# A spare weight load moved ahead of a lot's last loads, its split placed behind later products, and no spare pairs in the second layer

## The chip, the cores and the metric

The kernel runs on one core of a Trainium2 chip. A time is the device time of one execution of the whole program in microseconds (us). Times of a kernel are the median of several executions; one more execution was profiled.

## The reference

The reference is an encoder trunk of two layers on 512 tokens of width 1024, all in fp32:

```
for i in range(DEPTH):                       # DEPTH = 2
    h = rms_norm(x, g_mix_pre[i])
    proj = h @ w_in[i]                       # queries, keys, values, memory queries
    ...                                      # layer 0: banded attention, layer 1: full attention
    o = jnp.concatenate([tok, mo], axis=-1) @ w_o[i]
    x = x + rms_norm(o, g_mix_post[i])
    h = rms_norm(x, g_ffn_pre[i])
    gu = h @ w_gate_up[i]                    # 1024 x 5632
    f = (jax.nn.silu(gu[..., :D_FF]) * gu[..., D_FF:]) @ w_down[i]     # D_FF = 2816
    x = x + rms_norm(f, g_ffn_post[i])
```

## The kernel before

**Products.** TensorE (PE) has to reach fp32 accuracy from fp32r operands, so every operand is split into a high part (ScalarE, ACT, line 318, here called `whi` for weights) and a low part (VectorE, DVE, line 322, `wlo`), and each product is three matmuls: high by high, low by high, high by low. A weight of 512 KB is loaded by the queue of SyncE (SP) into a tile of 128x1024, named `raw`, `ru` or `rb` by its pool, and split from there; `rs` is a half of that size.

**The feed-forward part** (`ffn`, line 984) runs over 22 blocks of 128 hidden columns in four lots, `LOTS` = 0-2, 2-8, 8-14, 14-22. The two lots of six blocks (`SEVEN`; here the first and the second lot of a layer) save multiplications by the scheme that makes a 2x2 block product from seven products. For each hidden block, `body` (line 1151) makes gate and up (PE lines 1131 to 1133); its end is `s` (DVE line 1185), which `keep_hidden` splits into the pair `f` (ACT line 1007, DVE line 1008), the stationary operand of the down product.

**The down product of such a lot** (`down`, line 1310; matmuls on lines 1257 to 1259) needs seven combinations of the four blocks b11, b12, b21, b22 of the down weight. `down_load` (line 1269) loads them in four steps, each as a main tile and an `rs`; sums are made by accumulating DMAs on GpSimd's (POOL's) queue: t1 = b11+b12, t2 = b22+t1, t3 = b12+b22, t4 = b21+t2. Step 0 and step 1 are issued during the lot's last two blocks, step 2 (t3) with the first product A11, step 3 (t4 and b22) after A12. In `down` follow six products of 18 matmuls each: A12 (with b21), S2 (t2), S1 (t1), S3 (t3), S4 (b22), A22 (t4). Each has six steps of three matmuls; the last hidden block enters A12 in its fifth step. Before each, `pairs` splits the main tile and the `rs`.

**Spare work.** Some weights of layer 1 are used once as they are, so layer 0 splits four of them ahead and stores the parts to DRAM, where the mixer of layer 1 reads them back (`unit` looks them up in `self.pairs`). The list is `self.todo`, set at line 1554: four query weights and then four output weights. Twice in each `down`, `spare` either takes the next weight, loads it and splits it in two halves into tiles `c` (high) and `s` (low), or stores the parts that the call before made. `ahead` (line 231), called four times in `ffn_out`, does the same with whole tiles. In layer 0, four calls of each kind make the pairs of the four query weights. The list isn't emptied, so in layer 1 the same calls load, split and store the four output weights, which nothing reads afterwards.

**Who sets the order.** PE's order is that of the code. The orders of ACT, DVE, POOL and SP are set by the tile framework's planner when the kernel is built, from the data's dependences and its own estimate of when they are ready; each of these engines then runs its list strictly in that order. `queue` ties the DMAs that it issues to each other, so that they keep the code's order on their queue. `raw` tiles have three buffers.

Of the kernel before, what the change touches and what calls it, by code (L numbers as in the profile page):

```python
# [203 lines left out]
class Trunk:  # L204
# [290 lines left out]
    def rope(self, l, x, t, n, z):  # L495
        return self.rope_b(x, t, n, z) if l else self.rope_a(x, t, n)
# [487 lines left out]
    def ffn(self, l, pools, forms, late, done):  # L984
# [3 lines left out]
        nc = self.nc  # L988
        f32r = lambda pool, shape, tag, n=1: pool.tile(shape, F32R, tag=tag, name=tag, bufs=n)
        F, o, gu, tmp = {}, [], pools["gu"], None  # L990
        w, raw, st, turn, kept, forms_due, ends = {}, {}, {}, {}, {}, [], {}

        def units(f):
            w[f] = [self.unit(self.a["wgu"][l, f, b]) for b in range(2)]
# [82 lines left out]
        def queue(eng, *args, **kw):  # L1077
            with self.tc.issue_after(ends[eng]) if eng in ends else nullcontext():
                ends[eng] = eng.dma_start(*args, **kw).ins
# [140 lines left out]
        for k in range(2):  # L1220
            c = slice(512 * k, 512 * k + 512)
# [30 lines left out]
        def times(ps, h, name, pr, steps, fresh):  # L1252
            mm = nc.tensor.matmul
            for i, t in steps:
                lh, ll = block(h["lot"], name, 0, i, t), block(h["lot"], name, 1, i, t)
                rh, rl = [pr[i // 2][z][:, i % 2 * 512:i % 2 * 512 + 512] for z in range(2)]
                mm(ps[t], lh, rh, start=fresh and i == 0, stop=False, skip_group_check=True)  # L1257
                mm(ps[t], lh, rl, start=False, stop=False, skip_group_check=True)  # L1258
                mm(ps[t], ll, rh, start=False, stop=i == HALF - 1, skip_group_check=True)  # L1259
# [27 lines left out]
            down_load(h, 2)  # L1287
            times(h["x"], h, "A11", h["w"], BY_UNIT[:4], True)

        def spare():  # L1290
            if l == 0 and "rope" not in turn:
                turn["rope"] = 1
                self.axial(tmp.tile([P, 10 * HD], F32, tag="rope", name="rope", bufs=1), queue, ends)
            if self.stores:
                for dst, src in self.stores:
                    queue(nc.sync, dst, src)
                self.stores = []
            elif self.todo:
                name, *at = self.todo.pop(0)
                x = self.wraw.tile([P, 1024], F32, tag="raw", name="raw", bufs=3)  # L1300
                queue(nc.sync, x, self.a[name][tuple(at)])
                self.pairs[(name, *at)] = y = [self.dram.tile([P, 1024], F32, name="pair", tag="_".join(map(str, (name, z, *at))))
                                               for z in range(2)]
                for z in range(2):
                    c = slice(512 * z, 512 * z + 512)
                    hi, lo = temp("c"), temp("s")
                    self.split(hi.bitcast(F32R), lo.bitcast(F32R), x[:, c])
                    self.stores += [(y[0][:, c], hi), (y[1][:, c], lo)]

        def down(h):  # L1310

            x = h["x"]
            due()
            out_of(x, 0, 0)
            w = pairs(h["b21"])
            z = [self.tagged("s"), self.tagged("s")]
            times(z, h, "A12", w, BY_UNIT, True)
            down_load(h, 3)
            spare()
            out_of(z, 0, 0)  # L1320
            w = pairs(h["t2"])
            times(x, h, "S2", w, BY_UNIT, False)
            out_of(x, 0, 1, True)
            w = pairs(h["t1"])
            y = [self.tagged("pv"), self.tagged("t")]
            times(y, h, "S1", w, BY_ROW, True)
            spare()
            out_of(y, 1, 1)
            w = pairs(h["t3"])
            times(x, h, "S3", w, BY_ROW, False)  # L1330
            out_of(x, 1, 1, True)
            w = pairs(h["b22"])
            times(y, h, "S4", w, BY_ROW, False)
            out_of(y, 0, 1)
            w = pairs(h["t4"])
            times(x, h, "A22", w, BY_ROW, False)
            out_of(x, 1, 0)

        for c, (f0, f1) in list(enumerate(LOTS))[1:]:
# [40 lines left out]
            if c in SEVEN:  # L1380
                down(head)
# [114 lines left out]
    def run(self):  # L1496
        tc, nc, a = self.tc, self.nc, self.a
        with ExitStack() as top:
            top.enter_context(tc.manual_schedule(engines={mybir.EngineType.PE}))
            glob = self.glob = self.pool(top, "glob")  # L1500
            self.small = self.pool(top, "small")
            self.wraw = self.pool(top, "wraw")
            self.whl = self.pool(top, "whl")
            self.ps, self.nbank, self.turns = self.psum(top, "ps"), 0, ["s0", "s1", "s2"]
            dram = self.dram = top.enter_context(tc.tile_pool(name="dram", bufs=1, space=bass.MemoryType.DRAM))
            xs = [[dram.tile([P, D], F32, name=f"x{i}{t}", tag=f"x{i}{t}") for t in range(NT)] for i in range(3)]
            self.spill = dram.tile([P, 2, KD, NMEM], F32, name="smem", tag="smem")
            x0 = [a["x"][0, t * P:(t + 1) * P] for t in range(NT)]
            out = [a["out"][0, t * P:(t + 1) * P] for t in range(NT)]

            cst = self.cst = glob.tile([P, 2 * P], F32, name="cst")
            self.ident = cst[:, :P]
            self.ropet = cst[:, P:2 * P].rearrange("p (a t d) -> p a t d", a=2, d=16)
            self.gcol = glob.tile([P, 2, KD], F32, name="gcol")
            self.sink, self.nsink = [glob.tile([P, NH], F32, name=z) for z in ("sink", "nsink")]
            self.gt = glob.tile([P, 2, 2, NT, HD], F32, name="gt")
            self.identr = glob.tile([P, P], F32R, name="identr")
            self.mhalf = glob.tile([P, 4], F32, name="mhalf")
            nc.gpsimd.memset(self.mhalf, -0.5)

            hs = [ExitStack() for _ in range(DEPTH + 1)]
            self.slab(hs[0], 0)
            hb, norm = ExitStack(), ExitStack()
            self.hbuf = self.pool(hb, "h0", side="right")
            self.norm_pool(norm)
            late = {}
            for l in range(DEPTH):
                last = l == DEPTH - 1
                mix = ExitStack()
                tokp = self.pool(mix, f"tok{l}")  # L1530
                core = ExitStack()
                mkp = self.pool(core, f"mk{l}")
                self.mT = tokp.tile([P, 2, KD, NMEM], F32R, tag="tok", name="mT", bufs=1)
                if l == 0:
                    late = self.start(mkp)
                norm.close()
                self.core = self.pool(core, f"core{l}")
                self.more = self.core if l else None
                self.mixer(l, mkp, late, tokp)
                self.more = None  # L1540
                core.close()
                hb.close()

                keep, fts, norm = ExitStack(), ExitStack(), ExitStack()
                if l == 0:
                    self.gap(keep, "gap0", 56)
                forms = Forms(self, self.pool(keep, f"keep{l}", side="right"),
                              self.pool(fts, f"forms{l}", side="right"))
                self.norm_pool(norm)
                self.hT = None  # L1550
                late = self.mix_out(l, forms, x0 if l == 0 else xs[1], xs[2 * l])
                mix.close()
                if not last:
                    self.todo = [("wq", 1, c, z) for c in (2, 3) for z in range(2)] + [("wo", 1, 0, u) for u in range(4)]
                ff = ExitStack()
                pools = dict(ff=ff, gu=self.pool(ff, f"gu{l}"), norm=norm, forms=fts)
                get, fs, o, head = self.ffn(l, pools, forms, late, keep.close)
                norm = ExitStack()
                if not last:
                    self.gap(hs[l + 1], "gap1", 8)  # L1560
                    self.slab(hs[l + 1], 1, side="right")
                    hb = ExitStack()
                    self.hbuf = self.pool(hb, f"h{l + 1}", side="right")
                self.norm_pool(norm)
                late = self.ffn_out(get, a["wd"][l], fs, o, head, a["g_ffn_post"][l], a["g_mix_pre"][1], xs[2 * l], out if last else xs[1], None if last else self.new_rs())
                ff.close()
                if l == 0:
                    hs[0].close()
            norm.close()
            for z in hs[:0:-1]:  # L1570
                z.close()
# [30 lines left out]
```

## Time and profile before

| | us |
|---|---|
| median of 3 executions | 1102.06 (1100.99 to 1105.8) |
| profiled execution, device time | 1100.04 |
| profiled execution, span from its first to its last instruction | 1098.3 |
| PE busy | 1065.9 (97%) |
| DVE busy | 899.5 (82%) |
| ACT busy | 697.7 (64%) |
| POOL busy | 251.8 (23%) |
| HBM read and written | 149.04 MB and 18.87 MB |
| mean granted clock of PE | 0.993 |

In the rows that follow, `A:B` is a stretch in us from the start of the span. In a row of such stretches stand its length, PE's busy time in it (with the number of matmuls that touch it), the granted clock (1.00 is full speed), the share of time in which the DMA engines were busy, and GB/s. A row of the timeline has an instruction's start, its duration, engine, source line, operation, what it writes and reads, and in square brackets the idle time of its engine before it with what ended it. `SPq` and `POOLq` rows are the issues of DMAs; q0 is the queue of POOL's DMAs and q1 that of SP's. A matmul starts 0.23 us after the one before it when nothing holds it; its row is longer since matmuls overlap.

### The profile page before, as it was taken

What the parts mean: (1) busy time and instruction counts of PE and PEld (TensorE: products, weight loads), DVE (VectorE), ACT (ScalarE), POOL (GpSimd) and SP (SyncE); (2) the same over time, 40 slices, a digit from 0 to 9 for tenths busy, and PEclk for the clock granted to TensorE, in tenths of its full rate; (3) what the DMA queues carried; (4) which work ended last, traced back from release to release, by engine and by line L of the source; (5) the groups of instructions that cost most, each with busy time, mean ns of one, the idle gap of its engine ahead of it and who ended that gap; (6) DMA issues with size and microseconds to landing.
All of it is one profiled execution on the core that took longest, in us unless ns stands there. A gap on an engine that the chain in (4) does not pass through costs nothing.

```text
span 1098.3 us, 20016 instructions
## 1 busy us (share of the span) xinstructions
PE 1065.9 (97%) x7364; PEld 973.1 (89%) x7364; DVE 899.5 (82%) x1567; ACT 697.7 (64%) x1435; POOL 251.8 (23%) x405
## 2 busy tenths in 40 slices
PE   9999999999989989999999999999999999999997
PEld 7899878999969979998898888778999799799986
DVE  7889876978978979985888998767979888899955
ACT  7679975766636645664557888756766456556641
POOL 5673331111221100001443543312011011100001
PEclk9999999999989999999999999999999999999999
DMA  8721008357967983328743200145469968943283
GB/s 327 261 75 41 22 20 288 116 135 209 221 226 188 231 254 105 116 91 317 240 159 116 77 17 24 39 165 194 94 172 230 267 160 238 223 164 104 72 281 115
DMA packets 57555, 175.51 MB, mean 160 GB/s; under 512 B 6641, under 2 KB 7025, under 8 KB 57329
## 3 DMA queue, kind: packets, MB, share of 16 engines
q1 hardware_dynamic: 47952, 152.86, 40.9%
q0 software_dynamic: 9216, 20.98, 11.3%
q8 instruction: 58, 0.95, 0.3%
q10 hardware_dynamic: 288, 0.40, 0.1%
q14 instruction: 41, 0.33, 0.1%
HBM read 149.04 MB, written 18.87 MB: 153 GB/s over the span
## 4 chain that ended last, share of the span: by engine, by line
PE 75%; DVE 9%; DMA 6%; ACT 4%; issue 2%; POOL 2%; SPq 0%; DVEq 0%; POOLq 0%; ACTq 0%
PE ps L1131 11%; PE ps L1132 11%; PE ps L1133 11%; PE ps L309 8%; PE ps L308 8%; PE ps L310 8%; PE tp L673 3%; PE ps L1258 2%; PE ps L1259 2%; PE ps L1257 2%; DVE wlo L322 2%; PE o L687 2%; DMA rs<-rs 2%; PE o L688 2%; PE s L612 1%
## 5 line engine op out<-in xcount | busy, mean ns | idle before, releaser
L318 ACT ACTIVATE whi<-raw 128x512 fp32r<-128x512 f32 (+3 forms) x186 | 145.8, 803 | 99.6 <-issue 24.7
L322 DVE TENSOR_TENSOR wlo<-raw,whi 128x512 fp32r<-128x512 f32 (+3 forms) x182 | 162.7, 910 | 37.1 <-ACT whi L318 36.5
L1132 PE MATMUL ps<-hrows,wlo 128*128 128x256 f32 x640 | 176.2, 275 | 0.0
L1131 PE MATMUL ps<-hrows,whi 128*128 128x256 f32 x640 | 176.2, 275 | 0.0
L1133 PE MATMUL ps<-hrows,whi 128*128 128x256 f32 x640 | 176.1, 275 | 0.0
L308 PE MATMUL ps<-whi,hrows 128*128 128x256 f32 (+2 forms) x432 | 143.8, 333 | 0.0
L309 PE MATMUL ps<-wlo,hrows 128*128 128x256 f32 (+2 forms) x432 | 137.8, 319 | 1.6 <-DVE wlo L322 1.5
L310 PE MATMUL ps<-whi,hrows 128*128 128x256 f32 (+2 forms) x432 | 137.8, 319 | 0.0
L1132 PE MATMUL ps<-a,wlo 128*128 128x256 f32 x480 | 132.1, 275 | 0.0
L1131 PE MATMUL ps<-a,whi 128*128 128x256 f32 x480 | 132.1, 275 | 0.0
L1133 PE MATMUL ps<-a,whi 128*128 128x256 f32 x480 | 132.1, 275 | 0.0
L1131 PEld LDWEIGHTS ps<-hrows,whi 128*128 128x128 f32 x640 | 120.2, 188 | 0.5
L1132 PEld LDWEIGHTS ps<-hrows,wlo 128*128 128x128 f32 x640 | 120.1, 188 | 0.5
L1133 PEld LDWEIGHTS ps<-hrows,whi 128*128 128x128 f32 x640 | 120.2, 188 | 0.0
L663 POOL TENSOR_SCALAR p<-p,rd 128x256 f32<-128x256 f32 (+2 forms) x128 | 77.4, 626 | 102.1 <-DVE rd L660 58.3
L1132 PEld LDWEIGHTS ps<-a,wlo 128*128 128x128 f32 x480 | 90.1, 188 | 0.2
L1131 PEld LDWEIGHTS ps<-a,whi 128*128 128x128 f32 x480 | 90.1, 188 | 0.2
L1133 PEld LDWEIGHTS ps<-a,whi 128*128 128x128 f32 x480 | 90.1, 188 | 0.0
L309 PEld LDWEIGHTS ps<-wlo,hrows 128*128 128x128 f32 x432 | 81.4, 188 | 7.3 <-DVE wlo L322 2.4
L310 PEld LDWEIGHTS ps<-whi,hrows 128*128 128x128 f32 x432 | 81.1, 188 | 5.5 <-DVE hrows L336 0.3
L308 PEld LDWEIGHTS ps<-whi,hrows 128*128 128x128 f32 x432 | 81.3, 188 | 5.1
L318 ACT ACTIVATE whi<-rb 128x1024 fp32r<-128x1024 f32 x56 | 59.5, 1063 | 27.0 <-PE ps L1259 18.5
(231 smaller groups left out, 2854.1 us busy)
## 6 DMA issues: line engine op xcount, KB each, us to landing
raw<-in_wgu_dram SPq DMA_DIRECT2D x48, 512.0 KB, 4.7
rb<-in_wgu_dram SPq DMA_DIRECT2D x40, 512.0 KB, 4.4
raw<-in_wo_dram SPq DMA_DIRECT2D x20, 512.0 KB, 3.6
raw<-in_wd_dram SPq DMA_DIRECT2D x18, 512.0 KB, 4.6
raw<-in_wq_dram SPq DMA_DIRECT2D x16, 512.0 KB, 4.9
rb<-in_ws_dram SPq DMA_DIRECT2D x16, 512.0 KB, 6.6
rs<-in_ws_dram SPq DMA_DIRECT2D x28, 256.0 KB, 5.4
xt<-x SPq DMA_DIRECT2D x12, 512.0 KB, 4.4
```

The source lines that it names most:

```text
L308: mm(out, lh, rh, start=first, stop=False)
L309: mm(out, lh, rl, start=False, stop=False)
L310: mm(out, ll, rh, start=False, stop=last)
L318: a = nc.scalar.activation(hi, src, AF.Copy)
L322: b = nc.vector.tensor_sub(lo, src, hi.bitcast(F32))
L663: self.pooled = nc.gpsimd.tensor_scalar(hd["p"][z][:, :n], hd["p"][z][:, :n], rd[:, z:z + 1], 1.0, op0=OP.mult, op1=OP.mult)
L673: nc.tensor.transpose(tp[:, z], hd["p"][i][:, jj * P:(jj + 1) * P], self.ident)
L687: nc.tensor.matmul(o[:, c0:c1], hd["v"](j), th, start=(j == 0), stop=False, skip_group_check=True)
L688: nc.tensor.matmul(o[:, c0:c1], hd["v"](j), tl, start=False, stop=last, skip_group_check=True)
L1131: mm(out, wh[:, s], rh, start=start and k == 0, stop=False, skip_group_check=True)
L1132: mm(out, wl[:, s], rh, start=False, stop=False, skip_group_check=True)
L1133: mm(out, wh[:, s], rl, start=False, stop=k == 3, skip_group_check=True)
```

## The change

`spare` is taken apart. `spare_load` issues the load of the next spare weight right after A12's products, ahead of step 3's loads; `rope` (tables for layer 1, in the first lot of layer 0 alone) stays behind them; `spare_pair` splits the loaded weight behind S1's products and issues its four stores at once, where before the split stood at the first call and the stores at the second. And the list is emptied before the feed-forward part of layer 1, so that neither `spare_load`, `spare_pair` nor `ahead` does anything there.

```
+        def spare_load():
+            if self.todo:
                 name, *at = self.todo.pop(0)
                 x = self.wraw.tile([P, 1024], F32, tag="raw", name="raw", bufs=3)
                 queue(nc.sync, x, self.a[name][tuple(at)])
+                spares.append((x, name, *at))
+
+        def spare_pair():
+            if spares:
+                x, name, *at = spares.pop(0)
...
                 for z in range(2):
                     c = slice(512 * z, 512 * z + 512)
                     hi, lo = temp("c"), temp("s")
                     self.split(hi.bitcast(F32R), lo.bitcast(F32R), x[:, c])
-                    self.stores += [(y[0][:, c], hi), (y[1][:, c], lo)]
+                    queue(nc.sync, y[0][:, c], hi)
+                    queue(nc.sync, y[1][:, c], lo)
...
             times(z, h, "A12", w, BY_UNIT, True)
+            spare_load()
             down_load(h, 3)
-            spare()
+            rope()
...
             times(y, h, "S1", w, BY_ROW, True)
-            spare()
+            spare_pair()
             out_of(y, 1, 1)
...
                 mix.close()
+                self.todo = []
                 if not last:
                     self.todo = [("wq", 1, c, z) for c in (2, 3) for z in range(2)] + [("wo", 1, 0, u) for u in range(4)]
```

PE's order is the same before and after. Those of the other engines aren't. In the first lot of layer 0, SP's queue changes as follows; `raw<-in_wq` is the spare query weight, `raw<-in_wgu` are gate weights of the next lot, the rows of `in_ws` are the down weight's blocks (the two rows at the top are t3, those below t4 and b22):

```order
 L1079 DMA rb<-in_ws_dram 128x1024
 L1079 DMA rs<-in_ws_dram 128x512
-L1079 DMA rb<-in_ws_dram 128x1024
+L1079 DMA raw<-in_wq_dram 128x1024
+L1097 DMA raw<-in_wgu_dram 128x1024
+L1079 DMA rb<-in_ws_dram 128x1024
+L1097 DMA raw<-in_wgu_dram 128x1024
 L1079 DMA rs<-in_ws_dram 128x512
 L1079 DMA rb<-in_ws_dram 128x1024
```

Three loads of 512 KB now stand among and ahead of step 3's loads; before, all three stood behind them.

On ACT, in the same place, the splits of the spare weight (`c<-raw`) move too. `whi<-rb` and the first `whi<-rs` belong to b21, for A12; `whi<-ru` and the next `whi<-rs` to t2, for S2; the second `whi<-ru` to t1, for S1; line 1184 and line 1007 make the lot's last hidden block and the high part of its pair:

```order
 L318 ACTIVATE whi<-rb 128x1024
 L318 ACTIVATE whi<-rs 128x512
+L318 ACTIVATE c<-raw 128x512
 L318 ACTIVATE whi<-ru 128x1024
 L1184 ACTIVATE s<-ps 128x256
 L318 ACTIVATE whi<-rs 128x512
 L1007 ACTIVATE f_4231<-s 128x512
+L318 ACTIVATE c<-raw 128x512
 L318 ACTIVATE whi<-ru 128x1024
 L318 ACTIVATE f_4238<-q 128x512
```

Before, both halves stood together behind the splits of t3, for S3. The planner has not put them behind S1, where the code has them, but ahead of S2's splits. DVE's list has its part of the first half at the same place, ahead of the last hidden block's line 1185:

```order
 L322 TENSOR_TENSOR wlo<-rs,whi 128x512
 L1178 TENSOR_TENSOR c<-ps,u_4129 128x256
+L322 TENSOR_TENSOR s<-raw,c 128x512
 L322 TENSOR_TENSOR wlo<-ru,whi 128x1024
 L1185 TENSOR_TENSOR s<-s,c 128x512
```

The second lot of layer 0 has the same rows on ACT and DVE, and on SP its query weight stands right behind the `rs` of t3. In both lots of layer 1 the loads, splits and stores of the spare weight are gone, and SP's queue has three gate weights of the next lot ahead of the `rs` of t3 (its second row; the first row is t3's main tile, the last four are t4 and b22):

```order
L1079 DMA rb<-in_ws_dram 128x1024
L1097 DMA raw<-in_wgu_dram 128x1024 x3
L1079 DMA rs<-in_ws_dram 128x512
L1079 DMA rb<-in_ws_dram 128x1024
L1079 DMA rs<-in_ws_dram 128x512
L1079 DMA rb<-in_ws_dram 128x1024
L1079 DMA rs<-in_ws_dram 128x512
```

Before, two of these gate weights stood behind the last of the `in_ws` rows and behind the spare weight, and the third behind its stores.

More of the change, by code (lines that the diff above doesn't have):

```diff
@@ L990, in ffn @@
         F, o, gu, tmp = {}, [], pools["gu"], None
-        w, raw, st, turn, kept, forms_due, ends = {}, {}, {}, {}, {}, [], {}
+        w, raw, st, turn, kept, forms_due, ends, spares = {}, {}, {}, {}, {}, [], {}, []
         def units(f):
@@ L1288, in down_begin, with rope @@
             times(h["x"], h, "A11", h["w"], BY_UNIT[:4], True)
-        def spare():
+        def rope():
             if l == 0 and "rope" not in turn:
@@ L1293, in spare, with spare_load @@
                 self.axial(tmp.tile([P, 10 * HD], F32, tag="rope", name="rope", bufs=1), queue, ends)
[L1294 to L1298, printed above, removed]
+        def spare_load():
+            if self.todo:
                 name, *at = self.todo.pop(0)
@@ L1301, in spare, with spare_pair @@
                 queue(nc.sync, x, self.a[name][tuple(at)])
+                spares.append((x, name, *at))
+        def spare_pair():
+            if spares:
+                x, name, *at = spares.pop(0)
                 self.pairs[(name, *at)] = y = [self.dram.tile([P, 1024], F32, name="pair", tag="_".join(map(str, (name, z, *at))))
@@ L1307, in spare @@
                     self.split(hi.bitcast(F32R), lo.bitcast(F32R), x[:, c])
-                    self.stores += [(y[0][:, c], hi), (y[1][:, c], lo)]
+                    queue(nc.sync, y[0][:, c], hi)
+                    queue(nc.sync, y[1][:, c], lo)
         def down(h):
@@ L1317, in down @@
             times(z, h, "A12", w, BY_UNIT, True)
+            spare_load()
             down_load(h, 3)
-            spare()
+            rope()
             out_of(z, 0, 0)
@@ L1326, in down @@
             times(y, h, "S1", w, BY_ROW, True)
-            spare()
+            spare_pair()
             out_of(y, 1, 1)
@@ L1552, in run @@
                 mix.close()
+                self.todo = []
                 if not last:
```

## The prediction

> **What bounds the kernel now.** First the page, then PE's list of waits over the whole span (who, for whom: total us, times, longest):
>
> ```profile
> span 1098.3 us, 20016 instructions
> PE 1065.9 (97%) x7364; PEld 973.1 (89%) x7364; DVE 899.5 (82%) x1567; ACT 697.7 (64%) x1435; POOL 251.8 (23%) x405
> ...
> PE ps L1258 <- DVE wlo L322: 8.1, 4, 2.9
> PE ps L1257 <- DVE o L1267: 4.0, 1, 4.0
> ```
>
> PE is the bound; its two largest waits, 12.1 us, are all in the down products (1257 to 1259) of the two layers' seven-product lots, where the spare work stands. Next the stretches of these four blocks of 108 matmuls (layer 0's first and second lot, layer 1's first and second), and one stretch without a wait:
>
> ```profile
> 294.46:326.72 32.26, 27.38 (x110) 0.89 0.77 246
> 388.25:417.88 29.63, 26.69 (x111) 0.94 0.78 231
> 853.38:882.01 28.63, 26.72 (x110) 0.94 0.90 257
> 943.53:971.41 27.88, 25.39 (x110) 1.00 0.84 245
> 298.85:307.02 8.17, 8.17 (x38) 1.00 0.79 171
> ```
>
> In the last, 36 matmuls start (the count takes in two at its edges): 0.227 us each, 24.5 us for 108. A12's 18 take 4.4 instead of 4.1 us in each block (the first ends at 298.85), which the change doesn't touch. So 24.8 is what a block takes without the other waits, and 7.5, 4.8, 3.8 and 3.1 us stand over it: 19.2 us, the most that can be won. Part of this isn't waiting but slow running behind it:
>
> ```profile
> 315.27:320.70 5.43, 4.56 (x10) 0.50 0.89 301
> 406.04:409.45 3.41, 3.41 (x9) 0.50 0.99 351
> 870.25:873.66 3.41, 3.41 (x10) 0.50 1.03 351
> ```
>
> Half the clock over 4.56, 3.41 and 3.41 us of work costs 2.3, 1.7 and 1.7 us. The fourth block, whose wait was 2.4 us, ran at 1.00; the third's was 1.9:
>
> ```profile
> PE ps L1258 <- DVE wlo L322: 1.9, 1, 1.9
> ...
> PE ps L1258 <- DVE wlo L322: 2.4, 1, 2.4
> ```
>
> What the waits hang on is seen in the chain that ended last (start, us, what), here in the first and the last block:
>
> ```profile
> 305.75 6.37 DMA raw<-in_wq_dram
> ...
> 953.20 3.79 DMA raw<-in_wo_dram
> ```
>
> The spare weight is loaded last, ACT runs its list in order, and so the splits of later products (behind S3 in the first block, S3's own low part in the others) wait until it has landed and has been split.
>
> **Layer 1: the spare work goes.** With it go that load, ACT's two splits and DVE's two from the lists. What is late next? S4 needs b22's second part, SP's last load, at its third step: 4.4 + 3 x 4.1 + 6 x 0.227 = 18.0 us after the block's start, at 871.4 and 961.6.
>
> ```profile
> 862.29 0.33 SPq L1079 DMA_DIRECT2D rs<-in_ws_dram  x1
> ...
> 952.82 0.33 SPq L1079 DMA_DIRECT2D rs<-in_ws_dram  x1
> ...
> rs<-in_ws_dram SPq DMA_DIRECT2D x1, 256.0 KB, 2.6
> ```
>
> (The third row is a DMA issue with its us to landing, the same load in layer 0's first block.) Landed after 2.6 and split in 1.3 (a high part of 128x512 and a low one, 0.6 and 0.7 in rows below), it is ready at 866.2 and 956.7, 5.2 and 4.9 us early. The three gate weights that now go ahead of t3's second part hold it up by 1.3 us each (below: 512 KB land 1.3 us after the load in front of them), 3.9 us: no new wait, if barely. So both blocks fall to 24.8: **-3.8 and -3.1, -6.9 us**. `ahead`'s two loads, splits and stores in layer 1 go as well; that is worth nothing, since PE doesn't wait there:
>
> ```profile
> 980.00:1050.00 70.00, 70.00 (x607) 1.00 0.34 112
> ```
>
> **Layer 0: the wait moves to A12.** The four pairs are still made. Their loads now go out ahead of step 3's, but the first halves of their splits stand ahead of S2's on ACT and ahead of line 1185 on DVE. So all hangs on when the query weight lands. The rows of SP, ACT and DVE in the first block, and of PE's fifth step of A12:
>
> ```profile
> 288.14 0.33 SPq L1079 DMA_DIRECT2D rs<-in_ws_dram  x1
> 291.51 0.33 SPq L1079 DMA_DIRECT2D rb<-in_ws_dram  x1
> ...
> 291.90 0.63 ACT L318 ACTIVATE whi<-rs 128x512 fp32r<-128x512 f32 x1 [1.68 <-PE ps L1259]
> 293.30 1.06 ACT L318 ACTIVATE whi<-ru 128x1024 fp32r<-128x1024 f32 x1 [0.77 <-PE ps L1133]
> 312.14 1.15 ACT L318 ACTIVATE c<-raw 128x512 fp32r<-128x512 f32 x2 [8.32 <-DMA raw<-in_wq_dram]
> ...
> 294.39 1.23 DVE L322 TENSOR_TENSOR wlo<-ru,whi 128x1024 fp32r<-128x1024 f32 x1 [0.45 <-ACT whi L318]
> 295.54 0.68 DVE L1185 TENSOR_TENSOR s<-s,c 128x512 f32<-128x512 f32 x1
> 297.08 0.68 DVE L1008 SCALAR_TENSOR_TENSOR f<-s,f 128x512 fp32r<-128x512 f32 x1
> ...
> 297.21 0.39 PE L1257 MATMUL ps<-whi,f 128*128 128x512 f32 x1
> 297.82 0.50 PE L1259 MATMUL ps<-whi,f 128*128 128x512 f32 x1
> ```
>
> The landings of the two SP loads, in their order, and of one that POOL had issued at 286.23 in front of them:
>
> ```profile
> rs<-in_ws_dram SPq DMA_DIRECT2D x1, 256.0 KB, 7.5
> ...
> rb<-in_ws_dram SPq DMA_DIRECT2D x1, 512.0 KB, 5.5
> ...
> rb<-in_ws_dram POOLq DMA_DIRECT2D x1, 512.0 KB, 9.2
> ```
>
> POOL's accumulating DMA lands at 295.4, SP's load of 288.14 at 295.7 and the next at 297.0: while the former ran, SP's got hardly anything. The query weight will be issued at about 288.5, between these two, and takes the second one's place: **landed at 297.0**. Bounds: 292.5 if it took 4 us, as in the second block now (from 398.26, below); 299.5 after 11.0, the slowest landing of such a load here. I take 297.0, the row of the same size, queue and stretch.
>
> ACT reaches the split at 292.5 and waits 4.5 us. Then t2's split starts 0.5 later (a half of 1.15 is 0.58), DVE's part of t2 1.1 behind it and line 1185 1.15 behind that (293.30, 294.39, 295.54): 297.0 + 2.8 = 299.8, 4.2 later than now. Line 1008 and PE's step, which now hold each other at 297.82, move by the same: PE stands for 4.2 us in A12. After such a wait I expect one spell of half clock as in two of the rows above, 1.7 us (the first block's took 2.3). Everything behind is covered: S4's last part is issued some 4 us later too, as POOL's sum in front of it moves with the extra loads, and PE has lost 4.2 by then. So 5.9 us stand over 24.8 in place of 7.5: **-1.6 us**, with ends of -7.5 (landed at 292.5) and +2.6 (299.5 and two spells: 6.7 + 3.4).
>
> The second block in the same way:
>
> ```profile
> 382.34 1.17 SPq L1079 DMA_DIRECT2D rb<-in_ws_dram  x1
> ...
> 389.33 0.69 DVE L1185 TENSOR_TENSOR s<-s,c 128x512 f32<-128x512 f32 x1
> ...
> rb<-in_ws_dram SPq DMA_DIRECT2D x1, 512.0 KB, 6.5
> ...
> 398.26 4.01 DMA raw<-in_wq_dram
> ...
> rs<-in_ws_dram SPq DMA_DIRECT2D x1, 256.0 KB, 11.0
> ```
>
> (The last is the slowest landing, issued at 829.45.) The query weight takes the place of the load at 382.34 and lands at 388.8; line 1185 starts at 391.6 instead of 389.33, and PE waits 2.2 us. A wait of 1.9 was followed by a half clock and one of 2.4 wasn't, so I take half of 1.7: 3.1 us in place of 4.8, **-1.7 us**, with ends of -4.8 and +5.4.
>
> On this the Trainium skill, "TensorE: Matmul & The Clock Gate", part 1, has a rule: the clock falls to half after an idle window of about 3.4 us. By it a wait of 2.2 us costs no clock and the sum is 0.85 us lower. The trace speaks against it: 1.9 us of waiting were enough in layer 1's first block.
>
> **Sum.** -3.8 - 3.1 - 1.6 - 1.7 = -10.2 us against the profiled execution's 1100.04 gives 1089.8. The median of the runs is 2.0 us above that execution; with the same offset the forecast is 1092 us, 0.9% faster. A measurement of this kernel can tell about 0.5% (5.5 us, 1096.5 or 1107.6) from no change.
>
> **Rivals.**
>
> *The load shares the engines and lands in time.* If SP's loads aren't served behind POOL's but beside them, the query weight lands near 292.5 and 386.4 (4 us) and all 19.2 us go: 1102.1 - 19.2 = 1083. For it: after 382 us and elsewhere both kinds of DMA were in flight together. Against it: the load issued at 288.14 took 7.5 us for 256 KB, where the same took 2.6 at 304.43. Chance 0.13. The Trainium skill, "DMA: Bandwidth & Descriptors", section "Queues, rings and completion order", would have it so: each engine goes round the queues that have work, packet by packet. The 7.5 us speak against it here.
>
> *The load lands last, and the kernel gets slower.* The place is A12 of layer 0's two blocks; the price is the landing. After 11.0 us it lands at 299.5 and 393.3, line 1185 starts 6.7 us late in both, and two spells of half clock follow: 10.1 + 10.1 in place of 7.5 + 4.8, +7.9, less layer 1's 6.9: 1103. It decides from about 10.5 us on. For it: three more loads share the stretch, and POOL's took 9.2. Against it: only one small load of SP's is ahead of it in the queue. Chance 0.05; 1107.6 would need 13 us, which no row reaches.
>
> *The waits in layer 1 stay.* If three gate weights hold the last loads up by 7 us rather than 3.9, S4 waits about 2 us in each block, with a spell of 1.7, and what is won there is lost: 1102.1 - 3.3 = 1099, no change. For it: the slack is 1 us. Against it: the gate weights' buffers come free, and they go out, 2 us and more ahead of t3's second part, and in the second block SP's queue stands idle before it. Chance 0.12.
>
> **How the numbers follow.** The forecast has 0.70. Around it the landing's half microsecond either way and one spell of half clock more or less in each of two blocks make about 1088 to 1096. The range, 1084 to 1098, takes in the upper half of the first rival and the lower half of the third. Faster by over 0.5%: nearly all of the forecast and the first rival, 0.80. Within 0.5%: the third, most of the second and the forecast's upper edge, 0.17. Slower: 0.03.
>
> **What would show it.** In layer 1's blocks: stretches of 25 us and no PE wait in 1257 to 1259. In layer 0's: stretches of about 30.7 and 27.9 us; PE's wait in A12's fifth step, not in S3 or S4; ACT's wait of 4.5 and 2.5 us for the query weight ahead of t2's split. A wrong forecast shows as a query weight landed before 294 (no wait in A12), or as S4 waiting in layer 1.

## The result and the profile after

The changed kernel takes 1088.97 us (median of four runs, 1087.81 to 1091.88), the kernel before, in its runs so far, 1103.72 us (four runs, 1100.99 to 1105.80). The ratio is 0.9872 with a 95% interval of 0.9839 to 0.9904. Measured once more beside later runs of the kernel before (the last experiment below), it was 0.9899 (0.9884 to 0.9913). So by these two measurements the change makes the kernel 1.0 to 1.3% faster; the forecast was 0.9%. The profiled execution took 1088.87 us, with a span of 1087.0; the sum of the prediction had 1089.8 for it.

First the page's head, then PE's list of waits, as for the kernel before:

```profile
span 1087.0 us, 19967 instructions
...
PE 1062.3 (98%) x7364; PEld 972.1 (89%) x7364; DVE 894.4 (82%) x1561; ACT 693.4 (64%) x1429; POOL 253.0 (23%) x405
```

```profile
PE ps L1257 <- ACT f L1007: 3.9, 2, 2.1
...
PE ps L1258 <- DVE wlo L322: 0.4, 1, 0.4
```

The 12.1 us of waits in the down products have become 4.3 us: two waits in line 1257 and a small one. The four blocks of 108 down products and the two spells of half clock (stretch, its length, PE's busy time with its matmuls, clock, DMA share, GB/s):

```profile
292.97:322.59 29.62, 26.93 (x110) 0.94 0.83 248
384.76:413.39 28.63, 26.67 (x110) 0.94 0.73 218
849.07:873.87 24.80, 24.80 (x110) 1.00 0.71 192
935.39:960.18 24.79, 24.79 (x110) 1.00 0.63 179
298.82:302.23 3.41, 3.36 (x8) 0.50 1.07 231
390.98:394.39 3.41, 3.41 (x10) 0.50 0.99 195
```

Layer 1's blocks (the third and fourth row) run without a wait, at full clock, in the 24.8 us of an unhindered block. Layer 0's went from 32.26 and 29.63 to 29.62 and 28.63 us. The differences are -2.64, -1.00, -3.83 and -3.09, together -10.6 of the 11.3 us by which the span fell. The remaining 0.7 us lie outside the blocks: the first block starts 1.5 us earlier, behind the same instructions, and 0.8 us of that is lost again in other stretches, 0.6 of it right behind the first block.

What is left in layer 0 is where it was forecast. ACT's two first halves of the spare split, with what they waited for:

```profile
293.83 0.63 ACT L318 ACTIVATE c<-raw 128x512 fp32r<-128x512 f32 x1 [2.79 <-DMA raw<-in_wq_dram]
...
385.33 0.63 ACT L318 ACTIVATE c<-raw 128x512 fp32r<-128x512 f32 x1 [2.50 <-DMA raw<-in_wq_dram]
```

And PE's matmul in A12's fifth step that pays for each:

```profile
298.00 0.50 PE L1257 MATMUL ps<-whi,f 128*128 128x512 f32 x1 [2.12 <-ACT f L1007]
...
389.49 0.50 PE L1257 MATMUL ps<-whi,f 128*128 128x512 f32 x1 [1.82 <-ACT f L1007]
```

ACT stands 2.8 and 2.5 us for the query weight, with t2's split and the high part of the last hidden block (line 1007) behind it in its list; PE stands 2.1 and 1.8 us for the latter. The small wait in line 1258 comes from another place, DVE's line 1109, a sum for the next lot's gate weights. DVE stands at it for such a weight to land, and t4's low part, for A22, is behind it in the list:

```profile
316.12 0.69 DVE L1109 TENSOR_TENSOR ru<-raw,rb 128x512 f32<-128x512 f32 x1 [2.83 <-DMA rb<-in_wgu_dram]
```

### The profile page after: what moved, and what is told of

Same layout as the page of the kernel before. It is cut to its first block, busy times and chain, and to the rows that moved or that the text cites. A ratio compares the mean times of both kernels' runs of the same rounds, so it can differ in the third digit from the quotient of the medians.

```text
span 1087.0 us, 19967 instructions
## 1 busy us (share of the span) xinstructions
PE 1062.3 (98%) x7364; PEld 972.1 (89%) x7364; DVE 894.4 (82%) x1561; ACT 693.4 (64%) x1429; POOL 253.0 (23%) x405
## 4 chain that ended last, share of the span: by engine, by line
PE 78%; DVE 9%; DMA 4%; ACT 4%; issue 2%; POOL 2%; SPq 0%; DVEq 0%; POOLq 0%; ACTq 0%
PE ps L1133 11%; PE ps L1131 11%; PE ps L1132 11%; PE ps L309 9%; PE ps L308 9%; PE ps L310 9%; PE tp L673 3%; PE ps L1259 3%; PE ps L1258 3%; PE ps L1257 3%; DVE wlo L322 2%; PE o L687 2%; PE o L688 2%; PE s L612 1%; PE s L613 1%
```

## The experiments

The theory is the prediction's: each layer's gain is its own; in layer 0 the wait has only moved, to where ACT comes to the spare split before the weight has landed. The rivals are that the extra loads hold up other loads, that the move helps by itself in both layers, or that something else becomes late next. "Tied behind" means that the planner is told to put an instruction behind another one in an engine's list.

**The emptied list alone.** The kernel before, with one line added:

```diff
                 mix.close()
+                self.todo = []
                 if not last:
```

> The kernel before with one part of the change alone: layer 1's list of spare weights is emptied, so layer 1 loads, splits and stores none; in layer 0 the spare work stands as before. Theory (the two parts act each in its own layer and add): layer 1's two blocks of 108 down products fall from 28.6 and 27.9 to 24.8 us with no PE wait, layer 0's stay at about 32.3 and 29.6; the time falls by 6.9 us, 0.6%. Rival (the three gate loads that now stand ahead of the last down loads take the place of the spare load): PE waits about 2 us in the fifth product S4 of layer 1's blocks, these stay over 27 us, and the time falls by under 3 us.

Measured: 1093.26 us (1091.65 to 1095.26), ratio 0.9921 (0.9898 to 0.9945), by the ratio 8.7 us less than the kernel before (1101.38 in the runs beside it). Its four blocks:

```profile
293.12:326.53 33.41, 27.35 (x110) 0.90 0.76 224
388.04:418.20 30.16, 26.59 (x110) 0.94 0.77 227
853.27:878.11 24.84, 24.84 (x111) 1.00 0.76 204
939.63:964.48 24.85, 24.85 (x111) 1.00 0.58 161
```

Layer 1 is free. Layer 0 waits in the same places as before, its blocks 1.2 and 0.5 us longer. The theory holds; three gate loads ahead of the last down loads cost nothing. (6.9 us lie within the interval, 6.1 to 11.2, though near its end.)

**The move alone.** The changed kernel without that line:

```diff
                 mix.close()
-                self.todo = []
                 if not last:
```

> The changed kernel without the emptied list: the load stands ahead of step 3's loads and the splits behind S1 in the code, and layer 1 still makes its spare pairs. Theory: layer 0's blocks are those of the changed kernel (29.6 and 28.6 us, a wait of about 2 us in A12's fifth step and a half-clock spell); layer 1's blocks now show the same wait in A12's fifth step, 1.5 to 2.5 us with a spell of 1.7 or none, 26.5 to 29 us each; against the kernel before 3 to 6 us less, 0.3 to 0.5%. Rival (the move is what helped layer 1 too): layer 1's blocks take 24.8 us and the time is that of the changed kernel, 1.0 to 1.3% under before.

Measured: 1098.94 us (1096.0 to 1103.42), ratio 0.9978 (0.9960 to 0.9997), 2.4 us less than before. Its blocks, and two neighbouring stretches of 3.41 us that are used further down:

```profile
293.69:322.48 28.79, 26.50 (x110) 0.94 0.83 258
384.65:413.21 28.56, 26.78 (x111) 0.94 0.73 218
848.37:876.27 27.90, 25.40 (x111) 1.00 0.81 249
937.92:967.24 29.32, 27.03 (x110) 0.94 0.72 223
387.54:390.95 3.41, 1.63 (x7) 1.00 1.06 281
390.95:394.37 3.42, 3.42 (x10) 0.50 1.02 202
```

In layer 1 the move alone brings nothing: 27.90 and 29.32 us in place of 28.63 and 27.88. The wait in S3 has gone and one in A12 has come, as in layer 0 (0.9 and 1.6 us); that rival falls. A second wait has come in A22, 1.4 us in layer 1's first block and 0.5 in its second, which the expectation did not have:

```profile
PE ps L1258 <- DVE wlo L322: 1.9, 2, 1.4
```

In both, DVE stands at line 1109 until a gate weight has landed (3.5 and 2.6 us); the place comes up again in the next run. The gain was a little under the 3 to 6 us that were expected, and the last block a little over its 29 us. The two parts multiply to 0.9899, what the whole change gave when it was measured again. Most of its gain is work that layer 1 no longer does.

**The spare splits behind S1's.** The changed kernel, the spare splits tied behind t1's on ACT and DVE (they then stand right behind them, ahead of t3's):

```diff
-                self.split(hi[:, :n], lo[:, :n], x)
+                turn["split"] = self.split(hi[:, :n], lo[:, :n], x)
...
-                    self.split(hi.bitcast(F32R), lo.bitcast(F32R), x[:, c])
+                    with self.tc.issue_after(turn["split"][0]), self.tc.issue_after(turn["split"][1]):
+                        self.split(hi.bitcast(F32R), lo.bitcast(F32R), x[:, c])
```

> The changed kernel with the spare splits tied behind the splits of t1 in the lists of ACT and DVE, where the code has them; loads and their order are nearly the same. Theory (what is left in layer 0 is ACT standing at the spare split, ahead of t2's, until the query weight has landed): the PE wait of 2.1 and 1.8 us in A12's fifth step and both half-clock spells go, all four blocks take 24.8 us, 8.6 us less than the changed kernel: about 1080 us. Rival (the extra loads hold up the down weights' own blocks, t2 among them): the wait in A12 or S2 stays, a block takes 28 us or more, and the time is within 3 us of the changed kernel. Second rival (the splits are late again for S3): PE waits in S3 as before the change, 2 us or more a block.

Measured: 1088.09 us (1086.91 to 1090.52), ratio 0.9876 (0.9848 to 0.9904): no better than the changed kernel. The wait in A12 has gone with its cause, so the first half of the theory stands. But the 8.6 us didn't come, since a third place became late, which none of the expectations had. Layer 0's blocks, DVE's rows at the end of the first, and PE's wait for them:

```profile
293.13:323.26 30.13, 26.43 (x110) 0.94 0.80 240
384.78:411.77 26.99, 25.08 (x110) 1.00 0.74 221
```

```profile
314.78 0.69 DVE L1109 TENSOR_TENSOR ru<-raw,rb 128x512 f32<-128x512 f32 x1 [5.42 <-DMA rb<-in_wgu_dram]
315.51 0.69 DVE L1110 TENSOR_TENSOR rb<-rb 128x512 f32<-128x512 f32 x1
316.12 0.68 DVE L1267 TENSOR_TENSOR o<-o,ps 128x512 f32<-128x512 f32 x1
316.71 1.22 DVE L322 TENSOR_TENSOR wlo<-rb,whi 128x1024 fp32r<-128x1024 f32 x1
```

```profile
PE ps L1258 <- DVE wlo L322: 5.6, 2, 3.7
```

DVE stands 5.4 us at line 1109 until the gate weight has landed. t4's low part (line 322), for which A22's second matmul waits, stands behind it. PE waits 3.7 and 1.9 us there. In the changed kernel the same place cost PE 0.4 us, with DVE standing 2.8: its wait in A12 and the half clock behind it had held up PE's block, and so given the weight more time.

**The query weight loaded one step earlier.** The changed kernel, the load ahead of step 2's:

```diff
             h["w"] = pairs(h["b11"])
+            spare_load()
             down_load(h, 2)
...
-            spare_load()
             down_load(h, 3)
```

> The changed kernel with the query weight loaded one step earlier, ahead of t3's loads instead of behind them. The spare split's first half stands one place earlier still on ACT, ahead of the small split of b21. Theory (the landing alone sets the wait): the load is issued about 10 us earlier and has landed by the time ACT comes to it; the wait in A12 falls from about 2 us to under 0.7 (0.6 of it for the split itself), no half-clock spell, blocks of 24.8 to 25.6 us, and the time is 7 to 8.6 us under the changed kernel. Rival (loads pay for each other on the shared engines): t3 or b21 land later by what the query weight takes, PE waits in A11, A12 or S3 for 1 us or more, and half or more of the gain is lost.

Measured: 1089.22 us (1086.02 to 1092.40), ratio 0.9887 (0.9861 to 0.9914). Issued at 275.07, the weight landed 7.0 us later, at 282.1, and ACT came to it without a wait at 288.9; the wait in A12 is gone, so it was the landing that set it. PE waits 3.3 and 1.2 us in A22 instead, for the same line 1109, and a half-clock spell follows the first: blocks of 30.14 and 26.37 us. The theory had the wait in A12 right and the total wrong. The rival, that t3 or b21 come late, did not come about.

**The gate sums behind t4's splits.** The kernel with the splits behind S1's, and the sums of lines 1109 to 1111 tied behind t4's low split (and each unit's behind the last one's; `self.flo` is the instruction behind which they stand):

```diff
...
-            with self.tc.issue_after(forms.last[1] if f == 3 else self.flo) if f > 2 else nullcontext():
+            with (self.tc.issue_after(forms.last[1] if f == 3 else self.flo) if f > 2 else nullcontext()), (self.tc.issue_after(turn["sum"]) if "sum" in turn else nullcontext()):
...
-                nc.vector.tensor_add(ru[:, 512:], ru[:, :512], rb[:, 512:])
+                turn["sum"] = nc.vector.tensor_add(ru[:, 512:], ru[:, :512], rb[:, 512:]).ins
...
             w = pairs(h["t4"])
+            self.flo = turn["split"][1]
             times(x, h, "A22", w, BY_ROW, False)
```

> The kernel with the spare splits behind S1's, and on DVE the sums of the next lot's gate weights (lines 1109 to 1111) now tied behind the low splits of t4. Theory (in that kernel PE waits 3.7 and 1.9 us in A22 because DVE stands at line 1109 for a gate weight that lands late, with t4's low split behind it in the list): both waits and the half-clock spell go, all four blocks take 24.8 us, 7.5 us less than that kernel's 30.1 and 27.0, about 1080 to 1081 us. Rival (the gate weight is needed right behind the block anyway): PE waits as long in the next lot's first gate products, lines 1131 to 1133 and their like, and the time stays within 2 us of that kernel.

Measured: 1082.41 us (1080.67 to 1084.06), ratio 0.9835 (0.9813 to 0.9856): the fastest here, 1.7% under the kernel before, and its slowest run is below the changed kernel's fastest. Its blocks, and what remains in PE's list of waits behind the first of them:

```profile
293.02:317.81 24.79, 24.79 (x110) 1.00 0.88 275
380.94:405.77 24.83, 24.83 (x111) 1.00 0.84 259
842.22:867.02 24.80, 24.80 (x111) 1.00 0.80 211
928.76:953.57 24.81, 24.81 (x111) 1.00 0.64 179
```

```profile
PE ps L1131 <- ACT p L1137: 1.3, 1, 1.3
```

All four blocks run unhindered, layer 0's in 7.5 us less than in the kernel it builds on. The stretches behind layer 0's blocks grew by 2.7 us, 1.3 of them as this wait in the next lot's gate products, as the rival had it in part; by the spans (1085.1 and 1080.6) and by the ratios 4.5 us stay won. Against the changed kernel it is about 6 us (6.4 by the spans; 4.1 and 7.0 by its two ratios).

**The stores later.** The kernel with the splits behind S1's; a pair's four stores behind the next lot's first loads:

```diff
-                    queue(nc.sync, y[0][:, c], hi)
-                    queue(nc.sync, y[1][:, c], lo)
+                    self.stores += [(y[0][:, c], hi), (y[1][:, c], lo)]
...
+            for dst, src in self.stores:
+                queue(nc.sync, dst, src)
+            self.stores = []
             p1(gs[0])
```

> The kernel with the spare splits behind S1's, and the four stores of a spare pair queued behind the next lot's first gate loads; only in the first lot of layer 0 does this move them, in the second the order stays. Theory (the gate weight is late since four stores and their 1 MB stand ahead of it on SP): it is issued about 2 us earlier and lands 2 to 3.5 us earlier, the first block's wait in A22 falls from 3.7 to under 1.7 us with no half-clock spell, the block from 30.1 to 25 to 26.7 us, the second stays at about 27.0; 3.5 to 5 us less than that kernel. Rival (the loads are held by the engines being full, not by their place): the gate weight lands within 1 us of where it did, and so does the time.

Measured: 1088.62 us (1087.96 to 1089.26), ratio 0.9892 (0.9874 to 0.9910). The expectation failed. The gate weight was issued at 306.04 instead of 308.38, but took 8.4 us in place of 6.4 and landed at 314.40 instead of 314.76; PE waited 4.3 us in A22. The rival, that its place in the queue doesn't decide, fits the figures, but the run isn't a clean test of it. The new order also put another gate weight of 512 KB (line 1097) in front of this one, where it had stood behind it, so the 1 MB in front was halved and not taken away. And a table of 64 KB ahead of both (`rope`, issued at 305.03) landed 6.8 us after its issue, in place of 2.9. Why it did is open, and so is whether the place in the queue decides. PE waited 2.95 us in the second block, whose order was the same, and 1.9 there, so differences of 1 us in such a wait say little.

**Both earlier load and gate sums tied.** The kernel with the earlier load, with the tie of lines 1109 to 1111 as above:

```diff
...
             w = pairs(h["t4"])
+            self.flo = turn["split"][1]
             times(x, h, "A22", w, BY_ROW, False)
```

> The kernel with the earlier load of the query weight, and the gate sums tied behind t4's low splits in the same way. Theory: the waits of 3.35 and 1.2 us in A22 and the spell go, all four blocks take 24.8 us, 6.9 us less than that kernel, 1080 to 1083 us. Rival as for the first of these runs: the wait moves into the next lot's gate products, within 2 us of that kernel.

Measured: 1084.40 us (1082.62 to 1086.66), ratio 0.9855 (0.9834 to 0.9876). The blocks fell to 24.85 and 24.87 us; 2.9 us of waits turned up in the next lots' gate products. By the ratios about 3.5 of the expected 6.9 us came, half way to the rival. The second way of having the weight in time shows the same as the first: it pays only with the tie.

**The gate sums tied, nothing else.** The changed kernel with only that tie:

```diff
...
             w = pairs(h["t4"])
+            self.flo = turn["split"][1]
             times(x, h, "A22", w, BY_ROW, False)
```

> The changed kernel with the gate sums tied behind t4's low splits, and the spare split left where it was, ahead of t2's. Theory (the waits in A12 and in A22 stand one behind the other, and the first gives the gate weight the time to land): only the 0.4 us in A22 of layer 0's first block go; the A12 waits of about 2 us and both half-clock spells stay, blocks of 29.2 and 28.6 us, the time within 1.5 us of the changed kernel. Rival (the tie by itself brings what it brought together with the later split): 6 us less than the changed kernel.

Measured: 1087.46 us (1085.92 to 1087.91), ratio 0.9885 (0.9869 to 0.9902), beside 0.9899 (0.9884 to 0.9913) for the changed kernel on the same chip. The two are about 1 us apart, which these runs hardly tell from nothing and which is within the theory's 1.5 us. The waits in A12 stayed (2.2 and 2.4 us) and the one in A22 went. Only one of the two half-clock spells stayed, where the theory had both. Its blocks, and two stretches that are used below:

```profile
293.48:322.49 29.01, 26.70 (x110) 0.94 0.81 250
384.25:411.93 27.68, 25.09 (x111) 1.00 0.76 235
385.43:388.84 3.41, 1.73 (x8) 1.00 1.04 401
388.84:392.25 3.41, 2.51 (x10) 1.00 1.09 229
```

The tie alone is worth almost nothing, and so is the later split alone; only both together take off about 6 us. They are two waits one behind the other, of which the first hides the second.

**The changed kernel again**, unchanged:

> The changed kernel once more, beside the one above on the same chip. Every theory: 1087.8 to 1091.9 us as in its runs so far, 1.0 to 1.6% under before; layer 0's blocks show a wait of about 2 us in A12, layer 1's show none.

Measured: 1088.59 us (1087.90 to 1089.08), ratio 0.9899 (0.9884 to 0.9913). Layer 1's blocks were 24.8 us again; layer 0's took 28.38 and 30.54 us, with waits in A12 of 1.72 and 2.83 us (2.12 and 1.82 in the first profile) and one of 1.1 us in A22 of the first (0.4). ACT had stood 2.40 and 3.51 us for the query weight. The size of this wait changes from one execution to the next; its place doesn't.

## Why the prediction was right, and where its terms were off

**Layer 1, -3.8 and -3.1:** measured -3.83 and -3.09. "No new wait, if barely" was more comfortable than thought: the last load went out 11.0 us into the block, 2.1 later than before (862.29 - 853.38 = 8.9) and not 3.9, and landed 2.7 us on:

```profile
860.07 0.33 SPq L1079 DMA_DIRECT2D rs<-in_ws_dram  x1
```

With 1.3 us for the split it was ready at 864.1, 3 us ahead of S4's third step at 867.1. So the third rival had little chance; the emptied list alone shows the term by itself. That `ahead` is worth nothing was right too: the stretch behind the last block, in which it stands, took 126.9 us before and 126.8 after.

**Layer 0, first lot, -1.6:** measured -2.6. The mechanism, the place and the half-clock spell were right; the mis-sized term is the landing of the query weight. It was taken from the down load of 291.51 in the profile of before: 2.5 us into the block. It was 0.8 us into it here (293.81, against 292.97), so ACT waited 2.8 in place of 4.5 us and PE 2.1 in place of 4.2. The order of service was as supposed. The queues' packets, MB and share of the 16 engines, first from 287.1 to 290 us, while POOL's sum ran, then from 290 to 293.8:

```profile
q0 software_dynamic: 159, 0.52, 102.4%
```

```profile
q1 hardware_dynamic: 438, 1.36, 91.6%
q0 software_dynamic: 34, 0.07, 10.3%
```

From 287.1 to 290 only POOL's queue (q0) moves data, though SP's (q1) holds two loads; from 290 to 293.8 SP's has the engines almost alone. The first of the two, issued at 286.64, had its first packet 3.7 us later; the load issued at 305.16, with no packet of POOL's in its way, had it after 1.0. POOL's sum landed 3.3 us earlier than in the profile of before (292.13 against 295.44, 1.5 of it from the earlier start), and the weight followed it by 1.7. So the term was off because it was read from the place of one load, and not from when POOL's sum ends.

On this the Trainium skill, "DMA: Bandwidth & Descriptors", section "Queues, rings and completion order", says that an engine goes round its queues packet by packet. The rival that took it so had the landings 4 us after the issue; they took 6.8 and 6.5, and in the first block SP's queue got nothing for 2.7 us longer than with none of POOL's packets in its way. What was said for that rival, that after 382 us both kinds of DMA were in flight together, does not hold of their packets: in the profile of before POOL's queue alone moved data from 382 to 384.4 us, and SP's alone from 385 to 387.

**Layer 0, second lot, -1.7:** measured -1.0. The landing was right within 0.1 us (0.54 us into the block, 0.55 forecast), ACT's wait exactly (2.50), PE's 1.8 in place of 2.2. Off was the half spell put in: the spell came whole. Here the clock rule of the Trainium skill, "TensorE: Matmul & The Clock Gate", part 1, would have had none, as the prediction weighed; a wait of 1.82 us was enough.

**The sum, -10.2 us:** measured -10.6 in the blocks. Layer 1's two terms were right. In layer 0 the first term was 1.0 us too small and the second 0.7 too large, and that these nearly cancel is luck.

**"Everything behind is covered"** is the step that the prediction said too easily. In this kernel it failed by 0.4 us (1.1 in the second profile), and by no more only because the wait in A12 held PE up ahead of it. The first rival ("all 19.2 us go" when the weight lands in time) left out DVE's line 1109: with the weight in time and nothing else done, about 8.6 us more were due in the blocks, and no fall in the time can be told from the runs. As a bound, 19.2 us stands: with both waits gone the blocks lost just that (118.4 to 99.2 us), of which about 2.6 came back behind layer 0's.

**The offset of 2.0 us** from execution to median was not borne out: here the profiled execution is at the median. The kernel before ran from 1096.7 to 1107.2 us in its later runs; what was taken for an offset is their spread.

## What to carry to other kernels

When a wait is removed, ask of each engine's list what stands at its head for data, and what is queued behind it: here the weight's split on ACT and then a sum on DVE stopped work that was ready, and the first hid the second. A planner that knows no landing times may hoist work past the place where the code has it; read its order, and tie work that waits for a load behind work that doesn't. Work that nobody reads is the surest gain: one line gave about two thirds of this one (6.9 of 10.6 us in the blocks).

## What the hardware showed that was not expected

The half-clock spells, which the prediction had at "half a spell", follow a grid. But for the one in which each profile ends, all last 3.41 us or twice that, and begin and end a multiple of 3.41 us from one another. What decides is then not the wait's length but how much of one interval of this grid PE stood idle. Two intervals of the fourth block before, around its wait of 2.4 us; the third block's with its wait of 1.9 us stands ahead of them:

```profile
866.83:870.25 3.42, 1.51 (x7) 1.00 0.97 331
870.25:873.66 3.41, 3.41 (x10) 0.50 1.03 351
955.58:958.99 3.41, 2.25 (x10) 1.00 1.00 372
958.99:962.41 3.42, 2.18 (x10) 1.00 0.89 267
```

The wait of 1.9 us fell into one interval and left it 1.51 us busy: half clock in the next. The wait of 2.4 us was cut in two by the grid, 2.25 and 2.18 us stayed busy: no spell. Above, 1.63 us busy was followed by a spell (a wait of 1.64 us), and 1.73 wasn't (a wait of 2.44). That is a boundary near half of an interval. Two cases in the eleven profiles don't fit. The first two rows are of the kernel with the later stores, the others of the second profile of the changed kernel:

```profile
312.19:315.60 3.41, 1.53 (x7) 1.00 0.50 193
315.60:319.02 3.42, 0.96 (x4) 1.00 0.12 20
388.43:391.84 3.41, 2.78 (x7) 0.50 1.10 239
391.84:395.25 3.41, 3.41 (x10) 0.50 0.69 129
```

In the first, 1.53 us of work, with the wait at the interval's end, kept the full clock, and only the next interval brought the fall. In the second, 2.78 us of work at half clock did not end the spell, which went on for another interval. Both are open. The grid lies elsewhere in each execution: in the two profiles of the changed kernel, spells begin at 390.98 and at 388.43 us, 2.55 us apart, which is no multiple of 3.41. So a wait of about 2 us can cost 1.7 us more in one and nothing in another: the first block's, 2.12 and 1.72 us, was followed by a spell in the first profile and by none in the second. Part of the spread between runs of a kernel may come from that, which wasn't tried.
